# Where the tiles stand in on-chip memory: starts at multiples of 64 bytes, and other distances between a matmul's two operands, in a two-layer decoder trunk

## The chip, the cores and the metric

One core of a Trainium2 chip runs the whole program. The metric is the device time of one execution in microseconds; a run's figure is the median of several executions. On-chip memory (SBUF) has 128 partitions, and a tile takes the same bytes of each partition; "start" below means the byte in the partition at which a tile begins.

## What is computed

The reference is a decoder trunk of two layers over 256 tokens of width 1024, all in float32:

```python
for i in range(DEPTH):                     # DEPTH = 2
    x = x + 0.5 * swiglu(rmsnorm(x, ffn1_norm[i]), ffn1_w_gu[i], ffn1_w_down[i])
    h = rmsnorm(x, mix_norm[i])
    if kind == 0: y = nsa_mixer(h, ...)    # layer 0: compressed, selected and window attention
    elif kind == 1: y = swa_mixer(h, ...)  # layer 1: window-128 attention with sinks
    x = x + y
    x = x + 0.5 * swiglu(rmsnorm(x, ffn2_norm[i]), ffn2_w_gu[i], ffn2_w_down[i])
return rmsnorm(x, final_norm)
def swiglu(x, w_gu, w_down):               # D_FF = 2816
    g, u = jnp.split(x @ w_gu, 2, axis=-1)
    return (jax.nn.silu(g) * u) @ w_down
```

So there are six blocks: SwiGLU 0, the first mixer (`nsa`), SwiGLU 1, SwiGLU 2, the second mixer (`swa`), SwiGLU 3.

## The kernel before

**The split.** Each float32 operand of a large product is split into a high part in `float32r` and a low part that is the remainder; a product is the three matmuls high x high, high x low, low x high. Weights stream in from HBM in pieces of 128 x 1024 (`Weights.fetch`, tile `..._r`); ScalarE rounds a piece to its high part (`_h`, tag `whi`), VectorE or GpSimd subtracts for the low part (`_l`, tag `wlo`). Five raw pieces and four of each part are held.

**The two kinds of product.** A TensorE matmul has one operand that is loaded first, 128 columns at a time (LDWEIGHTS, engine PEld in the profile; below the *loaded* operand), and one that streams through (the *streamed* operand). While a matmul streams, the loaded operand of the next one is fetched.

- `gu`, the first half of a SwiGLU: the weights are loaded and the normed activations stream. `transposed` makes the activations, two k-blocks in one tile of tag `ahl` (names `xh...`), each k-block as 256 columns high and 256 low in one run. `product` issues for each k-block and each of gate and up a matmul of 512 columns (`gu_h` loaded; high and low stream together) and one of 256 (`gu_l` loaded): 16 such pairs for each of 22 blocks `f`, in each of four SwiGLUs.
- `dn`, the second half, and the mixers' projections `nin`, `nout`, `sin`, `sout` (`RowsProduct.block`): the activations are loaded (`hh`, `hl` in SwiGLU; `xh` or the heads' outputs `..._oh`, both tag `ahl`, in the mixers), and the weights stream, 512 columns wide in `dn` and `..out`, 256 in `nin` and `sin`. In SwiGLU 3 `dn` is cut 512, 256, 256 wide.
- In `nsa` there is one more product, `hid`, of 48 matmuls: compressed keys and values (`xh0`, `xl0`, `xh1`, `xl1` in `compress`) are loaded, and weight pieces `cmp_h`, `cmp_l` stream, 256 columns wide.

**Where tiles stand.** Pools hand out memory in the order in which tiles are made, each start rounded up to 32 bytes. The constants' pool comes first, then the weights' pool, the activations' pool `ap_`, the small pool `sp`, and each block's own pool, opened and closed with the block. The weight tiles are 4096 bytes, and all other large tiles are 512 bytes times a whole number, so that a family of tiles keeps its start modulo 512. Nothing in the kernel before sets that start. The table in the section on the change gives it.

**The order of work.** A Tile scheduler with priorities, two orders written out by hand (`NSA_STEPS`, `SWA_STEPS`) and tables of engines (`ENGINES`) set it. None of these is touched.

Of the kernel before, what the change touches and what calls it, by code (L numbers as in the profile page):

```python
# [13 lines left out]
F32 = mybir.dt.float32  # L14
F32R = mybir.dt.float32r
BF16 = mybir.dt.bfloat16
# [5 lines left out]
P = 128  # L22
D = 1024
S = 256
NT = S // P
# [5 lines left out]
NG = 4  # L31
# [1 line left out]
PIECE = 1024  # L33

BUFS = {
    "ra": 3, "rb": 2, "f2": 2, "ph": 5, "pl": 2, "qs": 2, "kk": 2, "vv": 8, "o_t": 5, "cm_e": 1, "cm_2": 14,
    "ahl": 5, "mx": 3, "sm": 3, "nm": 3, "ga": 2, "g0": 2, "u0": 2, "th": 2, "raw": 5, "whi": 4, "wlo": 4, "p4": 8,
}

# [1 line left out]

PAIR = {"nout": ('sc', 'tr'), "sout": ('sc', 'tr')}
PAIR_OTHER = ('out', 'sc')

ENGINES = {'hi_gu': 'A', 'lo_gu': 'V', 'hi_dn': 'A', 'lo_dn': 'VGVVVGGV', 'hi_nin': 'AAAAAAAAAAAAVAAA', 'lo_nin': 'VGGGVGGVVVGGVGVG', 'hi_cmp': 'A', 'lo_cmp': 'VVGVVVGVVGVVVVGG', 'hi_nout': 'AAAAAAAVVVAAAAAG', 'lo_nout': 'VG', 'hi_sin': 'A', 'lo_sin': 'GGGVVVGVVGGVGVVG', 'hi_sout': 'A', 'lo_sout': 'V', 'sqh': 'GAAVAAGGGAAAGGAA', 'sql': 'GGGVVVGVVGVGVVVG', 'qs': 'AVVAVAAAAAAAAAAA', 'kdh': 'VVVAVGGVGAGAAAAV', 'kdl': 'G', 'kk': 'A', 'ropeadd': 'GGGVVGGGVGGGVVGG', 'sc1': 'VVVVVVVVVVVVVAVV', 'sc2': 'VVAGVVGAVVVVGVVV', 'ph': 'A', 'tmp': 'A', 'oh': 'A', 'ol': 'VVVVVGVGGGGGVVVV', 'dup': 'VVVVAGGGAVVGAVVV', 'kca': 'AVAAAVVA', 'kcb': 'A', 'xr': 'VGGV', 'xhc': 'VVGAGVVAVGVVAVVV', 'xlc': 'GVGGVVGVGGGVVGVV', 'pc': 'AAVAAAAAVAAVVVVA', 'late': 'GGGVVGVGVGVGGGGG', 'xh': 'AAAVVVAVAVAVVVAV', 'ga': 'G', 'g0': 'A', 'u1': 'A', 'u0': 'G', 'hv': 'V', 'hh': 'AGVAGVGG', 'hl': 'GGGGVGGV'}

# [38 lines left out]
def trunk_kernel(tc, x_in, wgu, wdn, nsa_in, nsa_w1, nsa_out, swa_in, swa_out, small, fgain, consts, out):  # L85
# [3 lines left out]
    with ExitStack() as es:  # L89
        cp = es.enter_context(tc.tile_pool(name="const", bufs=1))  # L90
        wp = es.enter_context(tc.tile_pool(name="weights", bufs=1))
        ap_ = es.enter_context(tc.tile_pool(name="acts", bufs=1))
        sp = es.enter_context(tc.tile_pool(name="small", bufs=1))
        pp = es.enter_context(tc.tile_pool(name="psum", bufs=1, space=PSUM))

        cst = cp.tile([P, C_N], F32, name="cst")
        prm = cp.tile([P, D_N], F32, name="prm")
        x = [[cp.tile([P, 512], F32, name=f"x{t}{h}") for h in range(2)] for t in range(NT)]
        mhalf = cp.tile([P, NT], F32, name="mhalf")
        nc.gpsimd.memset(mhalf, -0.5)  # L100
        warm = cp.tile([P, NT], F32, name="warm")
        ident = cp.tile([P, P], F32, name="ident")

        def mm(o, w, m, start, stop):
            nc.tensor.matmul(o, w, m, start=start, stop=stop)  # L105
# [40 lines left out]
        class Weights:  # L146
# [27 lines left out]
            def get(self, c, n):  # L174
                b = max(k for k in self.parts if k <= c)
                hi, lo = self.parts[b]
                return hi[:, c - b:c - b + n], lo[:, c - b:c - b + n]


        def transposed(kp, norm, th, tl, tb, engine=None):  # L180

            ps = s_bank(f"xt{norm}_{kp}")
            for kk in range(2):
                for t in range(NT):
                    c = ((2 * kp + kk) % 4) * P
                    nc.tensor.transpose(ps[:, kk * S + t * P:kk * S + (t + 1) * P], x[t][kp // 2][:, c:c + P], ident)  # L186
            both = ap_.tile([P, 2, 2, S], F32R, tag="ahl", bufs=BUFS["ahl"], name=f"xh{norm}_{kp}")
            hi, lo = both[:, :, 0, :], both[:, :, 1, :]

            def evict(kk):  # L190
                k = 2 * kp + kk
                g = prm[:, D_GAIN + norm * KD + k:D_GAIN + norm * KD + k + 1]
                if (engine or pick("xh")) == "A":
                    nc.scalar.activation(hi[:, kk, :], ps[:, kk * S:(kk + 1) * S], AF.Copy, scale=g)  # L194
                else:
                    nc.vector.tensor_scalar(hi[:, kk, :], ps[:, kk * S:(kk + 1) * S], g, None, ALU.mult)
                nc.vector.scalar_tensor_tensor(lo[:, kk, :], ps[:, kk * S:(kk + 1) * S], g, hi[:, kk, :],
                                               ALU.mult, ALU.subtract)
                th[k], tl[k], tb[k] = hi[:, kk, :], lo[:, kk, :], both[:, kk, :, :].rearrange("p a t -> p (a t)")

            return evict
# [33 lines left out]
        class Norm:  # L235
# [18 lines left out]
            def first(self, wts, product):  # L254


                def load_x(h, queues):
                    for t, queue in enumerate(queues):
                        queue.dma_start(x[t][h], x_in[t * P:(t + 1) * P, h * 512:(h + 1) * 512])

                evict = {}

                def turn(*kps):
                    for kp in kps:
                        evict[kp] = transposed(kp, 0, self.h, self.l, self.both, "A")

                def leave(*ks):
                    for k in ks:
                        evict[k // 2](k % 2)

                zeros = ap_.tile([P, 512], BF16, name="zeros")
                nc.vector.memset(zeros, 0.0)
                ps = s_bank("idle")

                def multiply_zeros(n):
                    for _ in range(n):
                        mm(ps, zeros[:, :P], zeros, True, True)

                multiply_zeros(8)
                load_x(0, (nc.sync, nc.scalar))  # L280
                nc.scalar.dma_start(ident, consts[:, C_ID:C_ID + P])
                raw = [wts.fetch(o, n) for o, n in ((0, 256), (256, 768))]
                nc.scalar.dma_start(prm[:, :D_SINK], small[:, :D_SINK])
                load_x(1, (nc.sync, nc.scalar))
                raw += [wts.fetch(o, 512) for o in (1024, 1536)]
                nc.scalar.activation(warm, mhalf, AF.Exp)
                turn(0, 1)
                multiply_zeros(3)
                leave(0)
                wts.split(0, raw[0], 256, "AG")  # L290
                leave(2)
                product(0)
                wts.split(256, raw[1], 768, "AV")
                leave(1, 3)
                product(2)
                turn(2, 3)
                product(1, 3)
                leave(4)
                wts.split(1024, raw[2], 512, "AV")
                wts.split(1536, raw[3], 512, "GG")  # L300
                leave(6, 5, 7)
                product(4, 6, 5, 7)
                wts.load(CHUNK, CHUNK, engines="VG")
                for h in range(2):
                    squares(h, h * 512, h * 512 + 512, self.v, True)
                self.r = row_scale(self.v, "n0")
# [61 lines left out]

        def ffn(i, norm, nxt, residual=Residual):
            with tc.tile_pool(name=f"ffn{i}", bufs=1) as fp:  # L370
                wts = Weights(wgu[i], f"gu{i}")

                def banks(f):
# [15 lines left out]
                rb = fp.tile([P, S], F32, name="rb")  # L389
# [153 lines left out]
            tt("ol", ol[:, :, t * P:(t + 1) * P], o, oh[:, :, t * P:(t + 1) * P], ALU.subtract)  # L543

        def out_tiles(name):
            both = [ap_.tile([P, 2, 2, S], F32R, tag="ahl", bufs=BUFS["ahl"], name=f"{name}_oh{g}") for g in range(NG)]
            return [b[:, :, 0, :] for b in both], [b[:, :, 1, :] for b in both]

        def mask_of(t):
# [3 lines left out]
        def nsa(norm, nxt):  # L553
            with tc.tile_pool(name="nsa", bufs=1) as mp:
# [3 lines left out]
                qs = [mp.tile([P, 4, S], F32R, tag="qs", bufs=BUFS["qs"], name=f"qs{g}") for g in range(NG)]  # L558
                kk = [mp.tile([P, 2, 2, S], F32R, tag="kk", bufs=BUFS["kk"], name=f"kk{g}") for g in range(NG)]
                vv = [[mp.tile([P, 2, 2 * HD], F32R, tag="vv", bufs=BUFS["vv"], name=f"vv{g}{t}") for t in range(NT)]  # L560
                      for g in range(NG)]
                gate = mp.tile([P, NT, 3, NH], F32, name="gate")
                kc = [mp.tile([P, NG, KCW], F32, tag="p4", bufs=BUFS["p4"], name=f"kc{s}") for s in range(2)]
                kcs = mp.tile([P, NG, 2, NCP], F32R, name="kcs")
                vcs = mp.tile([P, NG, 2 * HD], F32R, name="vcs")
# [226 lines left out]
        def swa(norm, nxt):  # L792
            with tc.tile_pool(name="swa", bufs=1) as mp:
                tabs = rope_tables(norm, mp)
                nsink = mp.tile([P, NH], F32, name="nsink")
                nc.vector.tensor_scalar(nsink, prm[:, D_SINK:D_SINK + NH], -1.0, None, ALU.mult)
                qs = [mp.tile([P, 4, S], F32R, name=f"qs{g}") for g in range(NG)]
                kk = [mp.tile([P, 2, 1, S], F32R, name=f"kk{g}") for g in range(2)]
# [1 line left out]

                class Finish:

                    extra = 4

                    def __init__(self, g):
                        self.sink = nsink[:, 4 * g:4 * g + 4]

                    def before(self, pr):
                        nk = pr[0].shape[2] - 4
                        nc.gpsimd.tensor_copy(pr[0][:, :, nk:nk + 1], self.sink[:, :, None])  # L810

                    def least(self, hh):
# [53 lines left out]
        step(swa)  # L866
        with tc.tile_pool(name="last", bufs=1) as lp:
            fg = lp.tile([P, D], F32, name="fg")
            nc.scalar.dma_start(fg, fgain)
            end = Norm(6, LASTW)  # L870
            xg = {}
# [128 lines left out]
```

## Time and profile before

| | |
|---|---|
| median of 3 runs | 1018.31 us (1018.12 to 1018.9) |
| the profiled execution's own time | 1016.99 us |
| its span, first to last instruction | 1014.9 us |
| TensorE (PE) busy | 982.3 us, 97% |
| VectorE, ScalarE, GpSimd busy | 694.0, 556.3, 493.5 us |
| DMA | 169.10 MB, mean 167 GB/s |

A busy TensorE is no proof that it runs at its peak: the ends of matmuls are modelled, and they overlap. What one matmul takes from the next is read from the distance between starts (the *pace*).

### The profile page before, as it was taken

The page shows a single profiled execution, that of the slowest core. Times are in us where ns is not written, and L with a number is a line of the kernel's source. Part 1 is how long each engine was busy: PE and PEld are TensorE (multiplying, and loading weights), DVE is VectorE, ACT ScalarE, POOL GpSimd, SP SyncE. Part 2 cuts the span into 40 slices and gives each one's busy share as a digit, 9 for nine tenths or more (in the row PEclk, how much of TensorE's full clock was granted, in tenths as well). Part 3 has the DMA queues.
Part 4 walks back from the last instruction along what each step waited for, and adds up shares of the span by engine and source line. Part 5 has one row for each costly group of instructions (what it writes and reads, how often), then busy time and mean ns, then how long its engine had stood idle before and what let it go on. Part 6 is the DMA issues. An engine that isn't in the chain of part 4 may idle for free. (4 is left out here: it accounts for less than half of the span.)

```text
span 1014.9 us, 15910 instructions
## 1 busy us (share of the span) xinstructions
PE 982.3 (97%) x5626; PEld 845.8 (83%) x5626; DVE 694.0 (68%) x1299; ACT 556.3 (55%) x1041; POOL 493.5 (49%) x490
## 2 busy tenths in 40 slices
PE   7999999998899999999999999999999899999997
PEld 5888888887888788888888888888897688888897
DVE  6777754367788887778445877754179987877533
ACT  5555544446568755555444565544358755555442
POOL 2764563565354127555731555564562017555543
PEclk9999999998899999999999999999999999999999
DMA  8666666552421256666566666656552166666651
GB/s 279 198 194 187 184 188 189 171 165 74 135 84 57 81 154 191 185 203 186 183 185 197 172 201 189 187 167 218 176 164 84 49 204 202 187 186 191 189 184 42
DMA packets 47743, 169.10 MB, mean 167 GB/s; under 512 B 5424, under 2 KB 5808, under 8 KB 47664
## 3 DMA queue, kind: packets, MB, share of 16 engines
q1 hardware_dynamic: 46656, 166.43, 54.6%
q10 hardware_dynamic: 1008, 1.66, 0.4%
q8 instruction: 44, 0.72, 0.3%
q14 instruction: 35, 0.29, 0.1%
HBM read 167.02 MB, written 1.05 MB: 166 GB/s over the span
## 5 line engine op out<-in xcount | busy, mean ns | idle before, releaser
L105 PE MATMUL gu<-xh,gu_h 128*128 128x512 f32 x1408 | 490.7, 395 | 0.8 <-ACT xh L194 0.8
L105 PE MATMUL gu<-xh,gu_l 128*128 128x256 f32 x1408 | 390.4, 279 | 0.3 <-DVE gu_l L165 0.3
L105 PEld LDWEIGHTS gu<-xh,gu_h 128*128 128x128 f32 x1408 | 263.3, 188 | 61.8 <-ACT gu_h L139 1.3
L105 PEld LDWEIGHTS gu<-xh,gu_l 128*128 128x128 f32 x1408 | 264.6, 188 | 1.9 <-DVE gu_l L165 0.9
L165 DVE TENSOR_TENSOR gu_l<-gu_r,gu_h 128x1024 fp32r<-128x1024 f32 (+1 forms) x175 | 233.6, 1335 | 32.8 <-ACT gu_h L139 32.4
L139 ACT CAST gu_h<-gu_r 128x1024 fp32r<-128x1024 f32 (+1 forms) x177 | 184.1, 1042 | 45.6 <-PE gu L105 26.3
L139 ACT CAST dn_h<-dn_r 128x1024 fp32r<-128x1024 f32 (+1 forms) x89 | 92.2, 1041 | 106.2 <-PE dn L105 98.1
L105 PE MATMUL dn<-dn_h,hh 128*128 128x512 f32 (+1 forms) x396 | 145.7, 368 | 0.0
L105 PE MATMUL dn<-dn_h,hl 128*128 128x512 f32 (+1 forms) x396 | 145.6, 368 | 0.0
L105 PE MATMUL dn<-dn_l,hh 128*128 128x512 f32 (+1 forms) x396 | 145.4, 367 | 0.0
L165 POOL TENSOR_TENSOR dn_l<-dn_r,dn_h 128x512 fp32r<-128x512 f32 x66 | 90.0, 1385 | 100.4 <-ACT dn_h L139 100.0
L165 DVE TENSOR_TENSOR dn_l<-dn_r,dn_h 128x1024 fp32r<-128x1024 f32 (+1 forms) x56 | 71.1, 1274 | 98.2 <-ACT dn_h L139 98.2
L144 POOL TENSOR_TENSOR ga<-g,rb 128x256 f32<-128x256 f32 x88 | 96.0, 1091 | 62.3 <-DVE g L412 57.9
L144 POOL TENSOR_TENSOR hl<-u,hh 128x256 fp32r<-128x256 f32 x66 | 80.6, 1222 | 50.6 <-ACT hh L139 25.7
L144 POOL TENSOR_TENSOR u<-u,rb 128x256 f32<-128x256 f32 x88 | 69.5, 789 | 69.9 <-DVE u L414 68.0
L416 ACT ACTIVATE th<-ga 128x256 f32<-128x256 f32 x88 | 36.8, 418 | 91.3 <-POOL ga L144 90.5
L105 PEld LDWEIGHTS dn<-dn_h,hl 128*128 128x128 f32 x396 | 74.8, 189 | 12.5
L105 PEld LDWEIGHTS dn<-dn_l,hh 128*128 128x128 f32 x396 | 74.8, 189 | 12.4
L105 PEld LDWEIGHTS dn<-dn_h,hh 128*128 128x128 f32 x396 | 74.8, 189 | 12.2
L139 ACT COPY g<-gu 128x256 f32<-128x256 f32 x88 | 32.7, 372 | 86.9 <-PE gu L105 86.0
L105 PE MATMUL nin<-nin_h,xh 128*128 128x256 f32 (+1 forms) x320 | 65.4, 297 | 1.8 <-DVE r_b L445 1.6
L418 DVE SCALAR_TENSOR_TENSOR ga<-th,ga 128x256 f32<-128x256 f32 x88 | 42.8, 486 | 33.7 <-ACT th L416 33.6
(244 smaller groups left out, 1410.0 us busy)
## 6 DMA issues: line engine op xcount, KB each, us to landing
gu_r<-in_wgu_dram SPq DMA_DIRECT2D x174, 512.0 KB, 4.3
dn_r<-in_wdn_dram SPq DMA_DIRECT2D x87, 512.0 KB, 4.0
nin_r<-in_nsa_in_dram SPq DMA_DIRECT2D x18, 512.0 KB, 3.6
sin_r<-in_swa_in_dram SPq DMA_DIRECT2D x10, 512.0 KB, 3.6
nout_r<-in_nsa_out_dram SPq DMA_DIRECT2D x8, 512.0 KB, 3.6
sout_r<-in_swa_out_dram SPq DMA_DIRECT2D x8, 512.0 KB, 3.8
cmp_r<-in_nsa_w_dram SPq DMA_DIRECT2D x4, 512.0 KB, 4.3
nin_r<-in_nsa_in_dram SPq DMA_DIRECT2D x2, 456.0 KB, 4.2
```

The costliest lines, as they stand in the source:

```text
L105: nc.tensor.matmul(o, w, m, start=start, stop=stop)
L139: nc.scalar.copy(o, i)
L144: (nc.vector if pick(key) == "V" else nc.gpsimd).tensor_tensor(o, a, b, op)
L165: eng.tensor_tensor(lo[:, q:e], raw[:, q:e], hi[:, q:e], ALU.subtract)
L416: nc.scalar.activation(th, ga, AF.Tanh, scale=0.5)
L418: nc.vector.scalar_tensor_tensor(ga, th, 1.0, ga, ALU.add, ALU.mult)
```

## The change

No instruction is added, removed or moved: on every engine the list of instructions, their operands and their shapes are the same in the same order, and only the addresses differ. (One more wait stands in the list: VectorE's first sum of squares into `junk2` waits for VectorE's own clearing of `zeros`, since these now share a buffer. The rows of the window attention's probabilities `sa_p` lie 16 instead of 4 elements further apart than their length.)

- `fill` makes tiles that nothing reads, which shift what comes after them.
- The activations' tiles (tag `ahl`) become 512 bytes longer, and a block's data begins `PLACE` bytes into its tile: one number for each norm (`PLACE[0]` SwiGLU 0, `[1]` `nsa`, `[2]` SwiGLU 1, `[3]` SwiGLU 2, `[4]` `swa`, `[5]` SwiGLU 3), `PLACE_OUT` for the heads' outputs.
- `PLACE_H` shifts all tiles of a SwiGLU's own pool, `hh` and `hl` among them.
- The tag `cm_2` has 4 buffers instead of 14. Four tiles of it are made in all.

```diff
-    "ra": 3, "rb": 2, "f2": 2, "ph": 5, "pl": 2, "qs": 2, "kk": 2, "vv": 8, "o_t": 5, "cm_e": 1, "cm_2": 14,
+    "ra": 3, "rb": 2, "f2": 2, "ph": 5, "pl": 2, "qs": 2, "kk": 2, "vv": 8, "o_t": 5, "cm_e": 1, "cm_2": 4,
...
+PLACE = (64, 320, 192, 320, 192, 448)
+PLACE_OUT = (192, 192)
+PLACE_H = (64, 128, 256, 448)
...
+        def fill(pool, name, n):
+
+            pool.tile([P, n // 4], F32, name=f"fill_{name}")
+
+        fill(cp, "first", 896)
+        x = [[cp.tile([P, 512], F32, name=f"x{t}{h}") for h in range(2)] for t in range(NT)]
+        ident = cp.tile([P, P], F32, name="ident")
...
+        fill(cp, "const", 672)
+        fill(sp, "small", 320)
...
+        def split_tile(name, place):
+
+            t = ap_.tile([P, 4 * S + P], F32R, tag="ahl", bufs=BUFS["ahl"], name=name)
+            return t[:, place // 4:place // 4 + 4 * S].rearrange("p (k a t) -> p k a t", k=2, a=2)
...
-            both = ap_.tile([P, 2, 2, S], F32R, tag="ahl", bufs=BUFS["ahl"], name=f"xh{norm}_{kp}")
+            both = split_tile(f"xh{norm}_{kp}", PLACE[norm])
...
-                zeros = ap_.tile([P, 512], BF16, name="zeros")
+                zeros = ap_.tile([P, 512], BF16, tag="junk2", bufs=1, name="zeros")
...
+                if PLACE_H[i]:
+                    fill(fp, "place", PLACE_H[i])
...
-            both = [ap_.tile([P, 2, 2, S], F32R, tag="ahl", bufs=BUFS["ahl"], name=f"{name}_oh{g}") for g in range(NG)]
+            both = [split_tile(f"{name}_oh{g}", PLACE_OUT[name == "swa"]) for g in range(NG)]
...
+                fill(mp, "gate", 128)
...
+                fill(mp, "sink", 192)
...
-                    extra = 4
+                    extra = 16
...
+            fill(lp, "last", 704)
```

Starts modulo 512 bytes, from the built programs. "Distance" is the start of the loaded operand less that of the streamed one, modulo 512; a start of 480, 160, 32 or 288 is 32 more than a multiple of 64.

| product | loaded before | streamed before | distance before | loaded after | streamed after | distance after |
|---|---|---|---|---|---|---|
| `gu`, SwiGLU 0, 1, 2, 3 | 480 | 480 | 0 | 0 | 64, 192, 320, 448 | 448, 320, 192, 64 |
| `dn`, SwiGLU 0, 1, 2 | 160 | 480 | 192 | 64, 128, 256 | 0 | 64, 128, 256 |
| `dn`, SwiGLU 3 | 480 | 480 | 0 | 448 | 0 | 448 |
| `nin`, blocks of 256 columns | 480 | 480 | 0 | 320 | 0 | 320 |
| `nin`, the block of 304 columns | 480 | 480, 160, 352 in turn | 0, 320, 128 in turn | 320 | 0, 192, 384 in turn | 320, 128, 448 in turn |
| `sin` | 480 | 480 | 0 | 192 | 0 | 192 |
| `nout`, `sout` | 480 | 480 | 0 | 192 | 0 | 192 |
| `hid`, first half (`xh0`, `xl0`) | 288, 288 | 480 | 320 | 256, 256 | 0 | 256 |
| `hid`, second half (`xh1`, `xl1`) | 32, 288 | 480 | 64, 320 in turn | 0, 256 | 0 | 0, 256 in turn |

## Rows read from the trace of the kernel before

**Rows 1.** The profile's page: busy time of each engine, share of the span, instructions.

```profile
PE 982.3 (97%) x5626; PEld 845.8 (83%) x5626; DVE 694.0 (68%) x1299; ACT 556.3 (55%) x1041; POOL 493.5 (49%) x490
```

**Rows 2.** Waits of PE, the largest: us in total, times, longest.

```profile
PE r_q L460 <- POOL r_sq L144: 3.2, 2, 2.0
```

**Rows 3.** Windows, PE alone: busy (count of matmuls), granted clock, DMA share, GB/s.

```profile
30.00:130.00 100.00, 100.00 (x568) 1.00 0.63 186
380.00:480.00 100.00, 100.00 (x579) 1.00 0.65 191
560.00:660.00 100.00, 100.00 (x579) 1.00 0.64 187
835.00:935.00 100.00, 100.00 (x579) 1.00 0.65 194
```

**Rows 4.** Windows, every engine: PE, PEld, DVE, ACT, POOL, then clock and DMA.

```profile
380.00:480.00 100.00, 100.00 (x579) 87.49 (x578) 77.56 (x119) 56.23 (x97) 59.28 (x61) 1.00 0.65 191
...
197.00:318.00 121.00, 109.03 (x777) 100.37 (x775) 93.49 (x276) 75.94 (x193) 61.87 (x61) 0.94 0.35 105
```

**Rows 5.** Timeline of PE in `gu`: SwiGLU 0 (30:60), then SwiGLU 1 (400:430); start, duration.

```profile
29.77 0.40 PE L105 MATMUL gu<-xh,gu_h 128*128 128x512 f32 x1
...
59.80 0.40 PE L105 MATMUL gu<-xh,gu_h 128*128 128x512 f32 x1
...
399.83 0.40 PE L105 MATMUL gu<-xh,gu_h 128*128 128x512 f32 x1
...
430.00 0.39 PE L105 MATMUL gu<-xh,gu_h 128*128 128x512 f32 x1
```

**Rows 6.** Timeline of PE in `dn`: SwiGLU 1, SwiGLU 3 512 wide, SwiGLU 3 256 wide.

```profile
504.63 0.39 PE L105 MATMUL dn<-dn_l,hh 128*128 128x512 f32 x1
...
519.96 0.39 PE L105 MATMUL dn<-dn_h,hl 128*128 128x512 f32 x1
...
964.74 0.39 PE L105 MATMUL dn<-dn_h,hl 128*128 128x512 f32 x1
...
974.94 0.39 PE L105 MATMUL dn<-dn_h,hl 128*128 128x512 f32 x1
...
982.80 0.28 PE L105 MATMUL dn<-dn_l,hh 128*128 128x256 f32 x1
...
1002.96 0.28 PE L105 MATMUL dn<-dn_l,hh 128*128 128x256 f32 x1
```

**Rows 7.** Timeline of PE in `nin`: 304 wide, then 256 wide.

```profile
205.73 0.44 PE L105 MATMUL nin<-nin_h,xh 128*128 128x304 f32 x2
...
211.17 0.44 PE L105 MATMUL nin<-nin_h,xh 128*128 128x304 f32 x2
...
288.62 0.40 PE L105 MATMUL nin<-nin_h,xh 128*128 128x256 f32 x2
...
290.06 0.40 PE L105 MATMUL nin<-nin_h,xh 128*128 128x256 f32 x2
```

**Rows 8.** Timeline of PE in `hid`: first half, then from the second half on.

```profile
244.39 0.41 PE L105 MATMUL hid<-cmp_h,xl 128*128 128x256 f32 x1
...
246.95 0.41 PE L105 MATMUL hid<-cmp_h,xl 128*128 128x256 f32 x1
...
247.78 0.28 PE L105 MATMUL hid<-cmp_h,xl 128*128 128x256 f32 x1
...
249.14 0.28 PE L105 MATMUL hid<-cmp_h,xl 128*128 128x256 f32 x1
```

**Rows 9.** Timeline of PE: three matmuls of bf16 zeros; eight matmuls of 32 columns.

```profile
6.42 0.81 PE L105 MATMUL idle<-zeros 128*128 128x512 bf16 x3
...
279.17 1.07 PE L105 MATMUL cm_s<-kcs,qs 128*128 128x32 f32 x8
```

**Rows 10.** Tiles `zeros`, then `junk`, on DVE: min/median/max ns, first and last start.

```profile
L272 DVE MEMSET zeros<- x1: 272/272/272, 0.9 to 0.9; 128x256 uint32 x1
...
L213 DVE CUSTOM_DVE_ANT_0 junk<-x x2: 680/1232/1785, 15.5 to 18.4; 128x512 f32<-128x512 f32 x2
```

More of the change, by code (lines that the diff above doesn't have):

```diff
@@ L94, in trunk_kernel @@
         pp = es.enter_context(tc.tile_pool(name="psum", bufs=1, space=PSUM))
+        def fill(pool, name, n):
[3 more added lines that the diff above has]
+        ident = cp.tile([P, P], F32, name="ident")
         cst = cp.tile([P, C_N], F32, name="cst")
         prm = cp.tile([P, D_N], F32, name="prm")
-        x = [[cp.tile([P, 512], F32, name=f"x{t}{h}") for h in range(2)] for t in range(NT)]
         mhalf = cp.tile([P, NT], F32, name="mhalf")
@@ L101, in trunk_kernel @@
         warm = cp.tile([P, NT], F32, name="warm")
-        ident = cp.tile([P, P], F32, name="ident")
+        fill(cp, "const", 672)
+        fill(sp, "small", 320)
         def mm(o, w, m, start, stop):
@@ L808, in before @@
                     def before(self, pr):
-                        nk = pr[0].shape[2] - 4
+                        nk = pr[0].shape[2] - self.extra
                         nc.gpsimd.tensor_copy(pr[0][:, :, nk:nk + 1], self.sink[:, :, None])
```

## The prediction

> **What bounds the kernel now.** I read the page first: TensorE is busy 982.3 of 1014.9 us and no other engine above 694.0 [rows 1]. Then its waits: the largest sum behind one other instruction is 3.2 us [rows 2]. So the time is the number of matmuls times the pace at which they start, plus stalls in the two mixers. Next the windows: in a hundred microseconds inside SwiGLU 1, 2 and 3 TensorE passes 579 matmuls each time, inside SwiGLU 0 only 568, all at a granted clock of 1.00, the 2.4 GHz level [rows 3]; the other engines have room there, VectorE most used with 77.56 of 100 us, and DMA at a share of 0.65 [rows 4].
>
> The pace itself comes from starts in the timeline. First a floor. In `hid` at the 1.2 GHz level twelve matmuls of 256 columns take 246.95 - 244.39 = 2.56 us, 213.3 ns each [rows 8]: one column in each cycle and nothing lost. At 2.4 GHz that makes 106.7 ns for 256 columns and 213.3 for 512. Against this floor, the *excess* for each matmul:
>
> - `gu`, SwiGLU 0: 85 pairs of 512 and 256 columns in 59.80 - 29.77 = 30.03 us, 353.3 ns a pair; the floor is 320, so 16.7 ns a matmul [rows 5].
> - `gu`, SwiGLU 1: 87 pairs in 30.17 us, 346.8 a pair, 13.4 a matmul [rows 5]; SwiGLU 2 and 3 have the same count [rows 3].
> - `dn`, SwiGLU 1: 67 steps in 15.33 us, 228.8 ns, excess 15.5; SwiGLU 0 and 2 are built alike. SwiGLU 3: 45 steps in 10.20 us, 226.7; 168 steps of 256 columns in 20.16 us, 120.0: excess 13.3 in both [rows 6].
> - `nin`: 12 steps of 256 columns in 1.44 us, 120.0, excess 13.3; the block of 304 columns 39 steps in 5.44 us, 139.5 against a floor of 126.7, excess 12.8 [rows 7].
> - `hid` from the end of its first half on, at 2.4 GHz: 12 steps in 249.14 - 247.78 = 1.36 us, 113.3 ns, excess 6.7 [rows 8].
> - three matmuls of bf16 zeros, 512 columns: (0.81 - 0.38)/2 = 215 ns, excess 2 [rows 9].
>
> Two things are to be seen. The excess does not grow with the columns (13.3 for 256 and for 512), so it is paid once for each matmul and its load. And it is not the same everywhere: 6.7 where the loaded operand stands 64 or 320 bytes from the streamed one, 13.3 at distance 0, 15.5 at 192 (table of the change). It vanishes at the lower clock. That is what two reads of one memory that get in each other's way would look like, and the change moves just this distance.
>
> **The change part by part.** No instruction is added, removed or reordered, so every term is a number of matmuls times a difference of excess.
>
> The distance. After the change no large product stands at distance 0. `gu` in SwiGLU 1 and 3 and `nin` come to 320 or 64, the two that `hid` shows; the others to 64, 128, 192, 256 or 448. I take the excess of `hid`, 6.7, for all, since it is the only row with other distances and a settled pace, and the start at 64 (below) can only add to it. The terms: SwiGLU 0 `gu` 704 x (16.7 - 6.7) = 7.0 us; SwiGLU 1 to 3 2112 x (13.4 - 6.7) = 14.2; `dn` 0 to 2 792 x (15.5 - 6.7) = 7.0; `dn` 3 396 x 6.6 = 2.6. The mixers' projections are 480 + 240 + 192 = 912 matmuls, 6.0 us at 6.6 each, but TensorE idles 12 of 121 us in `nsa` [rows 4] and what it gains before a wait it gives back; I count half, 3.0. Sum 33.8 us.
>
> Starts at multiples of 64. Every operand of a large product stands at 32 more than a multiple of 64 now, so no row shows the other case. Bounds: nothing (the excess is the distance's alone), or all that is left of it, down to the zeros' 2 ns for 512 columns; for 256 columns not below 113.3, since eight matmuls of only 32 columns still start (1.07 - 0.26)/7 = 0.115 us apart [rows 9], which is the load. I take nothing for the point and keep the rest as a rival.
>
> The shared buffer of `zeros` and `junk2`: VectorE clears it at 0.9 us and writes the sum of squares at 15.5 at the earliest [rows 10], long after the last zero matmul of 6.42 us [rows 9]: nothing. `cm_2` has four buffers for four tiles: nothing. Longer rows of `sa_p`: the same elements, nothing. `fill` costs memory alone.
>
> Cover: a `gu` block of 16 pairs goes from 5.55 to 5.33 us, so VectorE's 77.56% becomes 81% and the DMA share 0.68 [rows 4]; neither becomes the bound.
>
> The profiled execution takes 1016.99 us; less 33.8 it is 983.2. The median is 1.3 above it, so 984 to 985 us; I say **984**.
>
> [...] Rows 6 give 228.8 ns at distance 192 and 226.7 at 0 for the same matmul, so the distance is seen. [...]
>
> **The rivals.**
>
> 1. *The excess goes almost whole* (distance and 64 bytes each hold a share). [...] Against: no row. A `gu` pair becomes 215.3 + 113.3 = 328.6: SwiGLU 0 352 x 24.7 = 8.7, the others 1056 x 18.2 = 19.2, `dn` 0 to 2 792 x 13.5 = 10.7, `dn` 3 132 x 11.4 + 264 x 6.7 = 3.3, projections half of 7.0: 45.4 us, 973 us.
> 2. *Only the distances shown to be good help.* 64 and 320 gain, the rest stays. For: `dn` is worse at 192 than at 0; the 304-column block, whose distance turns through 0, 320 and 128, has 12.8 and not 6.7 [rows 7]. SwiGLU 1 and 3 `gu` 1408 x 6.7 = 9.4, SwiGLU 0 `dn` 264 x 8.8 = 2.3, `nin` half of 3.2, less 704 x 2.2 = 1.5 for SwiGLU 2 `gu` at 192: 12 us, 1006 us.
> 3. *It does not do what it says*: the excess belongs to the instruction pair, and its steps (13.3, 15.5, 16.7) to how the pace happened to settle. [...] Against: six `dn` and `gu` stretches with one and the same value for one distance. 1018 us, give or take 2.
> 4. *Slower*: the new distances act as 192 does in `dn`, or the pace settles everywhere as in SwiGLU 0. 2112 x 3.3 = 7.0 in `gu` of SwiGLU 1 to 3, 396 x 2.2 = 0.9 in `dn` 3, 912 x 2.2 = 2.0 in the projections: 1028 us. It decides where a `gu` pair takes over 347 ns, or over 350 in two of the four SwiGLUs.
>
> **How the numbers follow.** Forecast 0.45, rival 1 0.17, rival 2 0.18, rival 3 0.10, rival 4 0.10. The range reaches from below rival 1 to above rival 2, which holds 0.8: 966 to 1010 us. A difference of 0.2%, 2 us, is about what a measurement of this kernel can tell from none. Faster by more: 0.45 + 0.17 + 0.18, and nothing of the rest, 0.80. The same: most of rival 3, 0.09. Slower: rival 4 and the rest of 3, 0.11.
>
> **What would show it.** In the changed kernel's timeline a `gu` pair takes about 333 ns in every SwiGLU (hundred microseconds hold about 600 matmuls), a `dn` matmul 220, `nin` 113. Pairs at 329 are rival 1; 333 in SwiGLU 1 and 3 but 346 or more in 0 and 2 is rival 2; 346.7 everywhere is 3; 350 and more is 4. The stalls of the mixers and the start should keep their sizes. The prediction is wrong at its root if the excess depends on something that the starts modulo 512 don't tell, as SwiGLU 0 against 1 warns.

## The result, and the profile after

The changed kernel takes **1022.73 us** (median of 20 runs, 1019.34 to 1024.76) against 1015.73 for the kernel before (20 runs beside them, 1012.74 to 1018.9): a ratio of **1.0062**, 95% interval 1.0051 to 1.0073. It is slower by 0.6%, where 984 us was forecast, and lies above the range. The rival that came is the fourth, "Slower".

The page of the changed kernel's profiled execution (span 1021.1 us, its own time 1022.93) counts as many instructions on each engine as [rows 1], with TensorE 4.3 us busier:

```profile
PE 986.6 (97%) x5626; PEld 845.9 (83%) x5626; DVE 697.0 (68%) x1299; ACT 558.1 (55%) x1041; POOL 484.2 (47%) x490
```

The windows of PE over the same four stretches as [rows 3], inside the four SwiGLUs (busy time, count of matmuls, granted clock, DMA share, GB/s):

```profile
30.00:130.00 100.00, 100.00 (x568) 1.00 0.64 186
380.00:480.00 100.00, 100.00 (x569) 1.00 0.64 188
560.00:660.00 100.00, 100.00 (x569) 1.00 0.63 183
835.00:935.00 100.00, 100.00 (x568) 1.00 0.64 185
```

SwiGLU 0 keeps its 568; the other three fall from 579 to 568 or 569. In these windows the granted clock is 1.00 in both kernels, and TensorE is busy throughout; its largest wait in the whole program is 3.5 us in sum, against 3.2 in [rows 2]. So it is the pace.

The timeline of PE in the changed kernel, first and last row of stretches without a gap: `dn` of SwiGLU 0 (distance 64, 87 steps), 1 (128, 70 steps) and 2 (256, 58 steps), then SwiGLU 3 (448), 512 wide (66 steps) and 256 wide (178 steps), two stretches of `nin` (320; 33 and 36 steps), and `gu` of SwiGLU 1 (320; 85 pairs):

```profile
139.68 0.39 PE L117 MATMUL dn<-dn_l,hh 128*128 128x512 f32 x1
...
159.98 0.40 PE L117 MATMUL dn<-dn_l,hh 128*128 128x512 f32 x1
...
505.61 0.39 PE L117 MATMUL dn<-dn_h,hh 128*128 128x512 f32 x1
...
521.88 0.39 PE L117 MATMUL dn<-dn_l,hh 128*128 128x512 f32 x1
...
685.81 0.39 PE L117 MATMUL dn<-dn_l,hh 128*128 128x512 f32 x1
...
698.96 0.39 PE L117 MATMUL dn<-dn_h,hl 128*128 128x512 f32 x1
...
959.82 0.39 PE L117 MATMUL dn<-dn_l,hh 128*128 128x512 f32 x1
...
974.93 0.39 PE L117 MATMUL dn<-dn_l,hh 128*128 128x512 f32 x1
...
984.76 0.28 PE L117 MATMUL dn<-dn_l,hh 128*128 128x256 f32 x1
...
1004.93 0.28 PE L117 MATMUL dn<-dn_h,hl 128*128 128x256 f32 x1
...
202.87 0.40 PE L117 MATMUL nin<-nin_h,xh 128*128 128x256 f32 x2
...
206.75 0.56 PE L117 MATMUL nin<-nin_h,xh 128*128 128x256 f32 x3
...
287.04 0.39 PE L117 MATMUL nin<-nin_h,xh 128*128 128x256 f32 x2
...
291.12 0.39 PE L117 MATMUL nin<-nin_h,xh 128*128 128x256 f32 x2
...
399.78 0.40 PE L117 MATMUL gu<-xh,gu_h 128*128 128x512 f32 x1
...
429.81 0.40 PE L117 MATMUL gu<-xh,gu_h 128*128 128x512 f32 x1
```

The paces of `dn` are 233.3, 232.4, 226.7, 228.9 and, 256 wide, 113.3 ns, so the excess over the floors of 213.3 and 106.7 is 20.0, 19.1, 13.4, 15.6 and 6.7. (A floor is half of what as many columns take at a granted clock of 0.50: 213.3 ns for 256 in [rows 8], and in the kernel before two steps of `na_o`, 512 wide, take 0.85 us from 256.23 us on, at 0.50. 256 columns in 213.3 ns are 1.2 a nanosecond, from which the prediction's 1.2 GHz, and 2.4 at a granted clock of 1.00, follow as an estimate if a column takes one cycle; no trace shows a frequency.) `nin` runs at 117.6 ns in the first stretch shown and at 113.3 in the second, with the same distance. Over all its 256-wide steps without a gap it takes 116.0 on average (119.3 before), and `sin` 116.1 (119.6 before). Beside [rows 6, 7]: what is **256 columns wide came down, to the 6.7 of the forecast in `dn` 3 and about half of the way in `nin` and `sin`; nothing 512 wide came down to 6.7**. The `gu` pairs take 353.3 ns (85 in 30.03 us), in all four SwiGLUs.

Stage by stage, from the first matmul of a stage to the first of the next (for the stages before a mixer and the last, to the last matmul), in us. The last column is `final`, the kernel at the end of the experiments:

| stage | before | after | forecast gain | gain | the last kernel |
|---|---|---|---|---|---|
| up to the first `gu` | 8.05 | 8.56 | 0 | -0.5 | 7.97 |
| `gu` 0 | 128.8 | 128.8 | 7.0 | 0.0 | 124.5 |
| `dn` 0 | 61.2 | 62.3 | 2.3 | -1.1 | 60.7 |
| first mixer | 168.7 | 167.8 | } 3.0 | 0.9 | 166.1 |
| second mixer | 86.8 | 86.4 | } | 0.5 | 86.6 |
| `gu` 1, 2, 3, each | 123.3 | 125.6 | 4.7 | -2.3 | 121.0 |
| `dn` 1 | 61.4 | 62.2 | 2.3 | -0.9 | 60.9 |
| `dn` 2 | 61.2 | 60.7 | 2.3 | 0.5 | 60.7 |
| `dn` 3 | 61.5 | 60.0 | 2.6 | 1.5 | 60.0 |

Between these two executions the whole loses 6 us (the medians differ by 7.0): 6.8 in `gu` 1 to 3, 2.0 in `dn` 0 and 1 and 0.5 at the start, less 3.3 gained elsewhere.

The first mixer's row holds more than the pace. In the nsa mixer the granted clock falls to 0.50 for short stretches, and not equally often in every execution: at about 227 to 230, 244 to 247, 254 to 257 and 268 to 271 us in the kernel before, at 228 to 231, 255 to 258 and 269 to 272 in the changed one. The window of the first mixer in the kernel before, the changed kernel, `shift32`, `nudge` and `final` (the last three are experiments below):

```profile
198.02:366.68 168.66, 155.11 (x1014) 0.96 0.34 104
199.68:367.46 167.78, 152.68 (x1013) 0.97 0.34 104
199.76:367.75 167.99, 154.06 (x1013) 0.96 0.34 104
199.03:365.18 166.15, 152.31 (x1013) 0.98 0.34 105
193.15:359.23 166.08, 151.23 (x1014) 0.98 0.35 106
```

`nudge` has every tile of the mixers where the kernel before has it, and takes 2.5 us less at 0.98 than at 0.96. At the same 0.96 the change's distances (`shift32`) gain 0.7 us, so part of the 0.9 in the table may be the clock's.

### The profile page after: what moved, and what is told of

It reads as the page before. It is cut to its first block, busy times and chain, and to the rows that moved or that the text cites. A ratio compares the mean times of both kernels' runs of the same rounds, so it can differ in the third digit from the quotient of the medians.

```text
span 1021.1 us, 15910 instructions
## 1 busy us (share of the span) xinstructions
PE 986.6 (97%) x5626; PEld 845.9 (83%) x5626; DVE 697.0 (68%) x1299; ACT 558.1 (55%) x1041; POOL 484.2 (47%) x490
## 3 DMA queue, kind: packets, MB, share of 16 engines
q10 hardware_dynamic: 1008, 1.66, 0.4%
## 5 line engine op out<-in xcount | busy, mean ns | idle before, releaser
L117 PE MATMUL gu<-xh,gu_h 128*128 128x512 f32 x1408 | 497.6, 397 | 1.3 <-ACT xh L211 1.3
L117 PE MATMUL gu<-xh,gu_l 128*128 128x256 f32 x1408 | 395.1, 282 | 0.3 <-DVE gu_l L177 0.3
L177 DVE TENSOR_TENSOR dn_l<-dn_r,dn_h 128x1024 fp32r<-128x1024 f32 (+1 forms) x56 | 73.7, 1321 | 98.2 <-ACT dn_h L151 98.2
L177 POOL TENSOR_TENSOR dn_l<-dn_r,dn_h 128x512 fp32r<-128x512 f32 x66 | 87.9, 1354 | 102.8 <-ACT dn_h L151 102.3
L156 POOL TENSOR_TENSOR ga<-g,rb 128x256 f32<-128x256 f32 x88 | 86.2, 980 | 64.7 <-DVE g L431 60.0
L156 DVE TENSOR_TENSOR u<-u,ga 128x256 f32<-128x256 f32 x88 | 38.1, 434 | 45.1 <-POOL u L156 42.2
```

The costliest lines, as they stand in the source:

```text
L156: (nc.vector if pick(key) == "V" else nc.gpsimd).tensor_tensor(o, a, b, op)
L177: eng.tensor_tensor(lo[:, q:e], raw[:, q:e], hi[:, q:e], ALU.subtract)
```

## The experiments

All move tiles alone, except `nudge`, which adds twelve small transposes, and `before2`, which changes nothing. "Excess" is meant for each matmul, as in the prediction. The theories, with the letters of the expectations: **D**, the distance sets the pace, but by another law for 512 columns than for 256; **A**, starts at multiples of 64 cost; **S**, the pace settles by chance, whatever the addresses. In the diffs below, `PLACE` and its two companions are written in one line.

**All distances 0, starts at multiples of 64** (`d0`), and **the change's own distances, all starts moved by 32 bytes** (`shift32`), part the two halves of the change.

```diff
 d0
+PLACE, PLACE_OUT, PLACE_H = (0,) * 6, (0, 0), (0,) * 4
 shift32
-        fill(cp, "first", 896)
+        fill(cp, "first", 928)
```

> All starts stay multiples of 64, but every large product stands at distance 0 again. Theory D (the distance sets the excess): gu pairs of SwiGLU 1 to 3 come back to 346.7 ns, dn 512 wide to 226.7 in all four SwiGLUs, dn 256 wide and the projections to 120.0; time about 1014 us, 1.7 under the kernel before. Rival A (the multiples of 64 cost it): gu pairs stay at 353.3 and the time near 1022. Rival S (the pace settles by chance, whatever the addresses): no order, single blocks at 346.7 or 353.3.

> All distances as in the changed kernel, all tiles moved on by 32 bytes, so that they start 32 past a multiple of 64 as in the kernel before. Theory D: every pace as in the changed kernel (gu pairs 353.3, dn 233.3, 232.4, 226.7, 229, dn 256 wide 113.3), time about 1022. Rival A: gu pairs back to 346.7 in SwiGLU 1 to 3, time about 1014. Rival S: no order.

`d0` ran at 0.9993 of the kernel before (95% interval 0.9981 to 1.0005), `shift32` at 1.0074 (1.0057 to 1.0091). `dn` of SwiGLU 0 in `d0` (80 steps):

```profile
141.64 0.39 PE L117 MATMUL dn<-dn_h,hl 128*128 128x512 f32 x1
...
159.78 0.39 PE L117 MATMUL dn<-dn_l,hh 128*128 128x512 f32 x1
```

and in `shift32` (78 steps):

```profile
141.62 0.39 PE L117 MATMUL dn<-dn_h,hh 128*128 128x512 f32 x1
...
159.82 0.39 PE L117 MATMUL dn<-dn_h,hh 128*128 128x512 f32 x1
```

226.8 and 233.3 ns. `shift32` repeats every pace of the changed kernel in `gu` and `dn`, the 113.3 of `dn` 3 and all four `gu` at 353.3 among them (`nin` and `sin` take 114.9 and 117.3 on average); `d0` repeats `gu` of before (568, 578, 579, 579 in the four windows). A is out: between these starts, the distance decides and the 64 bytes do not.

**Other distances.** Two kernels put each SwiGLU at distances not yet seen (the table `PLACE` and its two companions alone).

```diff
 scan_a
+PLACE, PLACE_OUT, PLACE_H = (256, 64, 128, 384, 448, 480), (64, 320), (320, 384, 32, 192)
 scan_b
+PLACE, PLACE_OUT, PLACE_H = (288, 384, 272, 416, 0, 352), (256, 128), (480, 96, 160, 224)
```

> Starts at multiples of 64 or 32, distances that no kernel had yet: gu 256, 384, 128, 32; dn 320, 384, 32, 192; nin 64, sin 448, nout 64, sout 320. Theory D: every distance has its own pace, gu between 333 and 360 a pair, 192 in dn 3 again 229 for 512 columns; dn 256 wide and nin, sin at any distance but 0 below 120. Rival S: gu pairs 346.7 or 353.3 in no order.

> More distances: gu 224, 240, 96, 160; dn 480, 96, 160, 224; nin 384, sin 0, nout 256, sout 128. Theory D with a period of 256 bytes (0 and 256, 64 and 320, 192 and 448 gave the same paces): dn at 480 as at 224, nout at 256 as at 0 (226.7), sout at 128 about 232, sin at 0 back at 120; gu at all four between 347 and 354 a pair.

One run each, 1022.44 and 1019.22 us. `dn` of SwiGLU 0 in `scan_a`, distance 320 (77 steps, 233.4 ns):

```profile
141.82 0.40 PE L117 MATMUL dn<-dn_l,hh 128*128 128x512 f32 x1
...
159.79 0.39 PE L117 MATMUL dn<-dn_h,hh 128*128 128x512 f32 x1
```

The excess by distance, read in this way from these two, the changed kernel, `d0` and the kernel before (`gu`: half of what a pair takes over 320 ns; most distances stand for one SwiGLU of one execution):

| distance | 0 | 32 | 64 | 96 | 128 | 160 | 192 | 224 | 256 | 320 | 384 | 448 |
|---|---|---|---|---|---|---|---|---|---|---|---|---|
| `dn`, 512 wide | 13.4 | 20.0 | 20.0 | 20.8 | 19.1 | 20.0 | 15.6 | 20.0 | 13.4 | 20.0 | 19.5 | 15.6 |
| `gu` pair | 13.3, 16.7 | 16.6 | 16.7 | 13.4 | 15.6 | 15.0 | 16.7 | 13.3 | 13.3 | 16.7 | 15.6 | 16.7 |

In `dn`, 512 wide, distances 256 apart agree within 0.4 ns: 0 with 256, 64 with 320, 128 with 384, 192 with 448, and 224 with 480 (20.0, `scan_b`). **There 0 and 256 are the best, not the worst**, and in `gu` nothing is better than 0 (96, 224 and, in `scan_b`, 240 are as good): the kernel before stood at the best distance in `gu` and in `dn` 3. At 256 columns the same move is a gain: 120.0 ns at 0, 113.3 or 117.8 at 448, 117.8 at 192. `hid`, which the change moved to 256 and 0, went the other way, from 113.3 to 120.0 ns (33 steps from 245.26 to 249.22 us). The row of `gu` is weaker than that of `dn`, since a pair can have two paces at one distance, as shown below for 0.

**Distances chosen by that table**: `gu` and `dn` 0 to 2 at 0, `dn` 3 at 448 and `nin` and `sin` as in the change (`mix`); and the change with `gu` alone back at 0 (`gu_back`).

```diff
 mix
+PLACE, PLACE_OUT, PLACE_H = (0, 320, 0, 0, 192, 0), (0, 0), (0, 0, 0, 448)
 gu_back
-PLACE = (64, 320, 192, 320, 192, 448)
+PLACE = (0, 320, 0, 0, 192, 0)
```

> The best pace seen so far for each product: distance 0 for gu, for dn 512 wide of SwiGLU 0 to 2 and for nout and sout, 448 for dn of SwiGLU 3 (256 wide at 113.3), 320 for nin, 192 for sin. Theory D: gains against the kernel before 792 x 2.2 = 1.7 us in dn 0 to 2, 264 x 6.7 - 132 x 2.3 = 1.5 in dn 3, 410 x 3.0 and 213 x 3.4 = 1.9 in nin and sin, of which half may be given back; 1011 to 1012 against 1015.7. Rivals A and S: no gain, 1016 or more.

> The changed kernel with only gu's four distances back at 0; dn, the projections and all else as changed. Theory D: gu pairs of SwiGLU 1 to 3 return to 346.7 ns (1056 pairs x 6.6 = 7.0 us less than the changed kernel), dn stays at 233.3, 232.4, 226.7 and 229 ns; time 1015 to 1016, the same as the kernel before. If gu is not the main price, the time stays over 1019.

`mix` came to 0.9971 (0.9952 to 0.9989; a median of 1013.69 us, where 1011 to 1012 was expected), `gu_back` to 0.9981 (0.9965 to 0.9998; 1013.72 us against 1015 to 1016): `gu` alone takes the change from 1.0062 to below the kernel before. Two things did not repeat. `gu` of SwiGLU 0 took 346.7 ns in `mix` (87 pairs), the first time that it did at distance 0:

```profile
29.63 0.39 PE L117 MATMUL gu<-xh,gu_h 128*128 128x512 f32 x1
...
59.79 0.39 PE L117 MATMUL gu<-xh,gu_h 128*128 128x512 f32 x1
```

And `dn` 3, 256 wide at 448, took 117.8 in both, where the change and `shift32` have 113.3.

**Two paces at one address** (`before2`, the kernel before again, and `nudge`, the kernel before with one, two and three transposes, into a bank that nothing reads, after blocks 6, 12 and 18 of SwiGLU 0 and 1).

```diff
+                    if i < 2 and f in (6, 12, 18):
+                        nudge = t_bank(f"nudge{i}_{f}")
+                        for n in range(f // 6):
+                            nc.tensor.transpose(nudge[:, n * P:(n + 1) * P], ident, ident)
```

> The kernel before once more, to see whether the pace of gu in SwiGLU 0 (353.3 ns a pair at distance 0, where SwiGLU 1 to 3 have 346.7) belongs to the program or to the execution. If to the program: 353.3 again. If to how the execution happens to settle: 346.7 in SwiGLU 0, or another block at 353.3.

> The kernel before with one, two and three transposes of 128 columns into an unused bank put in after blocks 6, 12 and 18 of gu in SwiGLU 0 and 1; not an address changes. If the two paces at distance 0 (353.3 in SwiGLU 0, 346.7 in 1 to 3) are two states into which the sequence settles after a disturbance, the pace jumps from one to the other behind some of the six places. If SwiGLU 0 has something else of its own, it stays at 353.3 and SwiGLU 1 at 346.7 behind all of them. Time within 3 us of the kernel before.

`before2` (1017.39 us) has 568, 579, 579, 579 again. In `nudge` (1016.85 us) the transposes begin at 53.0, 86.4 and 120.8 us in SwiGLU 0, at 405.3, 439.3 and about 473 in SwiGLU 1. Its `gu` rows between them, first and last of four stretches (75, 68, 43 and 86 pairs):

```profile
59.72 0.40 PE L105 MATMUL gu<-xh,gu_h 128*128 128x512 f32 x1
...
85.72 0.39 PE L105 MATMUL gu<-xh,gu_h 128*128 128x512 f32 x1
...
94.76 0.40 PE L105 MATMUL gu<-xh,gu_h 128*128 128x512 f32 x1
...
118.79 0.40 PE L105 MATMUL gu<-xh,gu_h 128*128 128x512 f32 x1
...
409.64 0.40 PE L105 MATMUL gu<-xh,gu_h 128*128 128x512 f32 x1
...
424.83 0.40 PE L105 MATMUL gu<-xh,gu_h 128*128 128x512 f32 x1
...
439.89 0.40 PE L105 MATMUL gu<-xh,gu_h 128*128 128x512 f32 x1
...
469.71 0.39 PE L105 MATMUL gu<-xh,gu_h 128*128 128x512 f32 x1
```

346.7, 353.4, 353.3, 346.7 ns, over the same tiles: the pace goes up after the transposes of 86.4 us, up after the one of 405.3, down after those of 439.3; the other three places leave it as it was. Already from 30 to 52 us, where its instructions are those of the kernel before, it is 346.6 against the 353.3 of [rows 5]. There the two executions differ in the clock. Both idle 2.5 us at the end of the norm, up to 23.1 us; then `nudge` (first row) has a granted clock of 0.50 and the kernel before (second row) 1.00:

```profile
23.89:27.30 3.41, 3.41 (x12) 0.50 1.00 366
23.89:27.30 3.41, 3.41 (x22) 1.00 0.94 344
```

`mix`, `scan_a` and `dn_loads` (below) have such a stretch there too, and a pair of SwiGLU 0 takes less behind it than ahead of the idle time (353 to 346.7, 353 to 346.7, 350 to 340 ns); in `gu_back` it takes more (346.7 to 353.3), and in the kernel before and `d0`, without it, more as well. So S is right in part: at distance 0 `gu` has two steady paces, and what comes before picks one; transposes do, and the stretch at the lower clock or the idle time ahead of it may. But S does not explain the change. Over the kernel before, its second profile, `d0`, `mix` and `gu_back`, 4 of 20 SwiGLUs at distance 0 had the slow one, all of them SwiGLU 0; at the change's distances, in the changed kernel and `shift32`, all 8 did. Whether those distances have a faster pace too, which no execution met, is not shown.

**High and low weights at different starts.** If 256-wide streams gain while their load stands at 448 and 512-wide ones want theirs at 0, `gu` can have both: `whi`, loaded while the 256-wide matmul streams (in the kernel before a load of `gu_h` and a 256-wide matmul both start at 30.01 us), moves, and `wlo` stays. `split` does that for all weights, `split_rev` the other way round (`HI, LO = 0, 448`, with other `PLACE` tables, so that the other operands come to a start of 0).

```diff
 split
+PLACE, PLACE_OUT, PLACE_H = (0, 64, 0, 0, 64, 0), (448, 448), (448, 448, 448, 384)
+HI, LO = 448, 64
...
+                if not count.get("apart"):
+                    fill(wp, "hi", HI)     # ahead of the first whi tile
...
+                    fill(wp, "lo", LO)     # ahead of the first wlo tile
```

> The high and the low weights get different starts: high at 448, low at 0, activations at 0. So a gu load that falls under the 512 wide matmul stands at distance 0, one that falls under the 256 wide matmul at 448. Theory D with the excess set by each stream and its own load: 13.3 after 512 columns and 6.7 after 256, a gu pair 340 ns, 9.4 us less in gu than at 346.7, time 1005 to 1008 against 1016. Rival P (the pair settles as a whole): 346.7 or more, time 1013 or more. dn has distances 0, 0, 448 in turn, expected between 226.7 and 228.9.

> The other way round in gu: the low weights, loaded under the 512 wide matmul, at distance 448; the high ones, loaded under the 256 wide one, at 0. By the same rule 15.6 + 13.3 over 320, a pair 349; rival P (only whether the distances are equal counts, not which load stands where): 340 as in split. dn has 0, 0, 64 in turn: no pace known, over 226.7.

`split` came to 0.9946 (0.9927 to 0.9966; 1010.7 us, where 1005 to 1008 was expected). Its `gu` in SwiGLU 1 (88 pairs, 340.0 ns, 226.7 + 113.3, as expected; SwiGLU 2 and 3 alike, SwiGLU 0 at 350.0):

```profile
399.75 0.39 PE L118 MATMUL gu<-xh,gu_h 128*128 128x512 f32 x1
...
429.67 0.39 PE L118 MATMUL gu<-xh,gu_h 128*128 128x512 f32 x1
```

`split_rev` (1018.2 us, one run) has `gu` pairs of 350.0, 351.1, 346.8 and 351.1, where 349 was expected and 340 by rival P: nothing won. So for a stream the load seems to count that falls under it, which is the load of the next matmul; if its own load counted, `split` would have the 349 and `split_rev` the 340.

`dn` missed in `split`: 232.0 ns, where 226.7 to 228.9 was expected. In `split_rev` it takes 228.9 in all four SwiGLUs (SwiGLU 1, 66 steps):

```profile
505.02 0.39 PE L118 MATMUL dn<-dn_h,hh 128*128 128x512 f32 x1
...
520.12 0.39 PE L118 MATMUL dn<-dn_h,hh 128*128 128x512 f32 x1
```

In both the loads of `dn` stand at one start and the streams change theirs from one matmul to the next, with distances 0, 0, 448 in `split` and 0, 0, 64 in `split_rev`. An average over the table's distances gives 213.3 + (2 x 13.4 + 15.6)/3 = 227.4 and 213.3 + (2 x 13.4 + 20.0)/3 = 228.9. So `split_rev` pays the average and `split` 4.6 ns more: changing starts of the streams alone do not explain the miss.

**Both, and the last two.** `best` also splits the mixers' activations and `hl`, so that in `dn` every stream meets distance 0 to the load under it, with the starts of both alternating (to its own load it stands at 448, 64 and 0 in turn). `final` goes back to `mix` and moves `whi` for `gu` alone. `dn_loads` is `final` with the start of `hl` alone moved, by 64, 192 and 256 in SwiGLU 0, 1, 2.

```diff
 best (split, and)
+PLACE = (0, 256, 0, 0, 256, 0)
+                        fill(fp, "hl", 64)     # ahead of the first hl tile
...
 final (mix, and)
-                hi = wp.tile([P, PIECE], F32R, tag="whi", bufs=BUFS["whi"], name=f"{self.name}_h{o}")
+                hi = wp.tile([P, PIECE + P], F32R, tag="whi", bufs=BUFS["whi"], name=f"{self.name}_h{o}")
+                c = 112 if self.kind == "gu" else 0
+                hi = hi[:, c:c + PIECE]
...
 dn_loads (final, and)
+                    if not f and i < 3:
+                        fill(fp, "hl", (64, 192, 256)[i])
```

> High and low weights at 448 and 0, gu's activations at 0, and now the loaded operands of dn, nin, sin, nout and sout follow with separate starts for their high and low parts, so that each stream meets one distance: dn 0 to 2 and both out projections 0, nin and sin 320, dn 3 448. Theory D with the excess set by each stream and its own load: gu pairs 340 in SwiGLU 1 to 3, dn 0 to 2 226.7 (split: 232), dn 3 256 wide 113.3 or 117.8, nin and sin about 116. Gain against the kernel before 7.0 + 1.2 in gu, 1.8 in dn 0 to 2, 0.3 to 1.5 in dn 3, about 1 in the projections: 1003 to 1005 against 1015.5. If dn stays at 232, the mixture of distances was not what split paid for.

> The high weights stand at 448 for gu alone and at 0 for all other products (their tiles are 512 bytes longer); low weights and gu's activations at 0; dn 0 to 2 and the out projections at distance 0, dn 3 at 448, nin 320, sin 192, with one start for high and low. So gu should be as in split and the rest as in mix. Theory D, with the excess set by the distances of the whole short sequence: gu pairs 340 in SwiGLU 1 to 3, 340 or 350 in SwiGLU 0, dn 0 to 2 226.7, dn 3 256 wide 113.3 or 117.8, nin and sin about 116; 1002 to 1006 against 1015.7. Rival: what split gained in gu it paid in dn for another reason than mixed starts, then dn stays at 231 and the time at 1007.

> As final, but in dn the loaded low parts hl begin at 64 (SwiGLU 0), 192 (1) and 256 (2) while the loaded high parts and all streamed weights stay at 0: distances 0, 0, d in turn, with only the loads changing their start. If each stream pays for its own load alone: 13.3, 13.3 and 20.0 / 15.6 / 13.3, so 228.9, 227.4 and 226.7 ns a matmul. If changing starts cost in themselves, as dn in best suggests (231 at distance 0 throughout), all three lie at 230 or more.

`best` came to 0.9927 (0.9902 to 0.9951; 1007.11 us, where 1003 to 1005 was expected), with all four `gu` at 340 ns, but `dn` 0 to 2 at 231.1 although every distance to the load under the stream is 0. `dn_loads` (1006.13 us, one run) has in `dn` of SwiGLU 0 (88 steps)

```profile
139.62 0.40 PE L117 MATMUL dn<-dn_h,hl 128*128 128x512 f32 x1
...
159.96 0.39 PE L117 MATMUL dn<-dn_h,hh 128*128 128x512 f32 x1
```

231.1 ns, as much again in SwiGLU 1, and 226.7 in SwiGLU 2. If each stream paid for the distance of the load under it alone, one load of three at 64 would give 228.9, as above, and one at 192 would give 227.4. So in these two kernels a load of `dn` whose start differs from that of the one before goes with a cost beyond the average, unless it differs by 256. That is not the whole law, since `split` pays beyond the average with all loads at one start. The law, and why `gu` pays nothing, stay open.

`final` is faster than both kernels: **1000.02 us** (999.82 to 1002.89; 1002 to 1006 was expected), a ratio of 0.9853 (0.9832 to 0.9873) to the kernel before (1015.62 beside it). Its windows, as [rows 3]:

```profile
30.00:130.00 100.00, 100.00 (x589) 1.00 0.64 191
380.00:480.00 100.00, 100.00 (x590) 1.00 0.63 190
560.00:660.00 100.00, 100.00 (x590) 1.00 0.65 193
835.00:935.00 100.00, 100.00 (x583) 1.00 0.66 195
```

The fourth window, 835 to 935, takes in the first matmuls of `dn`. By the stage table, 11.2 of the 17 us between the two profiled executions (15.6 between the medians) come from `gu` (4.3 of them from SwiGLU 0, which also lost its slow pace), 3.0 from `dn` and 2.8 from the mixers. The mixers' share is nearly all the clock's: at the same 0.98, `nudge` with the tiles of the kernel before takes 166.15 us in the first mixer and `final` 166.08.

## Why the prediction was wrong

**Right**: what bounds the kernel, that the pace depends on the distance, that the 64 bytes give nothing, and that the new wait and the longer rows cost nothing that shows (`d0` has them, at 0.9993). Of the 256-wide terms that of `dn` 3 held, at 113.3 ns.

**The step that failed** is "I take the excess of `hid`, 6.7, for all". Its reason was that `hid` is "the only row with other distances and a settled pace". It rested on "The excess does not grow with the columns", which the runs show at distances 0 and 256 alone: at 448, `dn` 3 of the changed kernel has 15.6 for 512 columns and 6.7 for 256. [rows 8] are 256 columns wide, and the 512-wide rows at hand, 15.5 at distance 192 against 13.4 at 0 [rows 6], already pointed the other way. The prediction read from those that the distance is seen, set them in rival 2, and then went by `hid` in the sum. Its own bound for 256 columns, the 0.115 us of [rows 9] taken as the load, is also a warning: 113.3 ns may be the pace of the loads, which would tell nothing of 512 columns. No run separates the two. At 512 columns `dn` had 13.4 to 20.0 at the change's distances, never 6.7, and the distance that the change left in `gu` and `dn` 3 was the best.

Term by term: `gu` 1 to 3 +6.8 us for -14.2, `gu` 0 nothing for -7.0, `dn` 0 to 2 +1.5 for -7.0, `dn` 3 -1.5 for -2.6, whose 132 matmuls of 512 columns went from 13.4 to 15.6. The mixers gave 1.4 us of 3.0, part of it perhaps the clock's. Half of that term was counted as given back before waits, but most of what is lacking was never gained: `nin` and `sin` fell by 3.3 and 3.5 ns where 6.6 was counted, and `nout` and `sout`, 512 wide, did not fall (229.4 and 229.2 to 229.4 and 230.0 on average).

**Rival 4** was right in kind and place: over 350 ns in four SwiGLUs, where it asked for two. Its 7.0 us for `gu` 1 to 3 came as 6.8. Its whole loss of 9.9 us, 1028 from the 1018.3 of three runs, stands against 7.0 from 1015.73: it let the 256-wide products lose as well, and they gained, and it left out what `dn` 0 and 1 lost. It had 0.10, though the observation that carried it, the 353.3 of SwiGLU 0, stood in the prediction as a warning.

**Rival 3** named a true thing: a pace can settle at either of two values at the same starts, 346.7 and 353.3 ns in SwiGLU 0 and 1 (`nudge`). It fails as an account of the change: `shift32` repeats its paces of `gu` and `dn`, and `gu_back` undoes those of `gu` 1 to 3.

**Still open**: what lies behind a period of 256 bytes in `dn` (the two reads of one memory that the prediction supposed are shown by no run); what picks one of the two paces; by which law changing starts cost in `dn`, and why not in `gu`.

## What to carry to other kernels

Where TensorE is the bound at a granted clock of 1.00, compare the distance between starts of matmuls with half of what as many columns take at 0.50 (here 213.3 ns for 512): a steady excess of 13 to 17 ns on each of 4916 matmuls of `gu`, `dn` and the projections, 64 us of the kernel before at 13 ns each, is worth an experiment on where tiles stand (15.6 us came of it here). A pace measured at one width must not be carried to another: here the same move took 2 to 6.7 ns from the 256-wide matmuls and put up to 6.6 on the 512-wide ones. Scan distances in one or two runs, one for each stage, before a layout is settled, and read a pace in more than one execution, since one layout can have two. Before a gain is put down to a stage, compare the clock granted in it: in the first mixer two executions with the same tiles lay 2.5 us apart, at 0.96 and 0.98.

## What the runs showed of the hardware that was not expected

- For `float32r` matmuls of 512 columns in `dn` the excess repeats with a distance of 256 bytes between loaded and streamed operand: 13.4 ns at 0 and 256, up to 20.8 between.
- The same instructions at the same addresses have two steady paces, 346.7 and 353.3 ns a `gu` pair, and one or two short transposes switch between them in either direction. 256-wide `dn` at 448 has 113.3 in four kernels (the changed one, `shift32`, `final`, `dn_loads`) and 117.8 in two (`mix`, `gu_back`); `nin` at 320 has both within one execution.
- With alternating starts of loads `dn` takes 231.1 ns a matmul against 226.7 (`best`, `dn_loads`), even where each stream meets distance 0, and `gu` pays nothing, where they bring the pair to 340. The paces of mixed distances are not always the average of their parts: 232.0 in `split` against 227.4, 228.9 in `split_rev` as computed.
